# An encoder layer on one core: dividing attention outputs, not probabilities, by the softmax's sums

## The chip, the cores and the metric

The kernel runs on one core of a Trainium2 chip. The metric is device time in microseconds (us) of one launch, and lower is better. Three runs of the kernel before gave 1881.48, 1882.19 and 1882.21 us; the median is 1882.19 us.

## What is computed

One encoder layer with shared weights is applied to two groups of 512 tokens (g = 0 and 1). Its parts are an RMSNorm and a combined input projection; a bidirectional mLSTM; a multi-head attention with low-rank queries and keys; a gated merge of the two branches with an output projection; a SwiGLU feed-forward block; a gated embedding; a last RMSNorm. The change lies in the attention: 8 heads of 128 + 64 columns over 512 tokens, in float32.

```python
def mla_attention(q_nope, q_rope, k_nope, k_rope, v):
    scale = (A_NOPE + A_ROPE) ** -0.5
    ...
    def one(args):
        qn, qr = args
        s = jnp.einsum('bqhd,bkhd->bhqk', qn, k_nope) + jnp.einsum('bqhr,bkr->bhqk', qr, k_rope)
        p = jax.nn.softmax(s.astype(jnp.float32) * scale, axis=-1).astype(v.dtype)
        return jnp.einsum('bhqk,bkhd->bqhd', p, v)
```

The queries come from `rmsnorm(c_q, g_q) @ w_uq`, so a factor on the normed `c_q` is a factor on all queries, rotated ones too.

## The kernel before, in words

Activations stand as tiles of 128 features by 512 tokens. Every float32 operand of a matmul is split into a high part (a cast by ScalarE, `S.copy`) and a low part (a subtraction, `lo_of`, L154, mostly by VectorE), and a product is three matmuls: high by high, high by low, low by high.

The stages follow each other: input projections and mLSTM up to about 550 us, attention from about 580 to 862 us, then the products "mo" and "ao" (mLSTM and attention outputs by their weights, L1090), the output projection, feed-forward and the end. Tiles of one stage are stored to DRAM and loaded back by the next one where they don't fit.

Attention runs over 8 heads, and in each over the two groups: 16 pairs (hd, g). `attn_proj` (L773) makes a pair's queries, keys and values one head ahead: `qn` and `kn` by matmuls into PSUM banks "pj", their high and low parts (`qnl`, `knl`), the values from DRAM (`avt`, L787), their low part `vnl` on GpSimd (L788). On even heads the rotary part (`rope`, L741) adds eight VectorE instructions per group for two heads. `attn` (L791) then takes four blocks of 128 queries:

- 5 matmuls give the scores `sc` of 128 queries by 512 keys (L799 to L803) in one of three PSUM banks.
- VectorE finds each row's maximum (L805) and multiplies it by minus the scale (L806); ScalarE takes the exponential with that as bias, and its sums (L808); VectorE inverts the sum (L809); then the 128x512 block `p` is multiplied by it, on ScalarE (L811), or in block 1 on VectorE (L813).
- TensorE transposes `p` in four pieces into one of two banks `pt` (L816), and the result is split into `aph` (ScalarE, L818) and `apl` (VectorE, L154).

After the fourth block 12 matmuls (L823 to L825) multiply with the values into the bank `av`, ScalarE copies it to the tile `oz` (L827), and SyncE stores that to DRAM (L828), where "ao" finds it after the four "mo" products.

What else shares the engines in this stage: the merge gates (`merge_gate`, L695: 48 matmuls each, tiles `tg`) beside heads 0 to 3, and beside heads 4 to 6 the "hops", the operands of the product "mo": for k = 0 to 3 four tiles of the mLSTM's output are loaded (`ld<-hzd`, L1026, L832), subtracted from each other (L862 on VectorE, L865 on GpSimd) and split (`xh` L884, `xl` L154). Beside head 7 sixteen such tiles are loaded once more for the later operands (L1060), added on GpSimd (L868, L874, L875).

The pool EV has two slots "ch" and two slots "bk" of 128x512. In this stage "ch" holds `oz`, "bk" holds the gates' `tg` and two of the four hop tiles of each k (`stage`, L1021). A slot is given again when its last reader is done.

The order on each engine is not the program's: a scheduler sorts all instructions at build time, by its own model of their durations (`schedule_with_timeline_sim`, L1527), and each engine then works through its list in that order and waits where an operand is not there. SyncE's list (SP) is that of nearly all DMAs: a DMA whose source is not ready holds up all behind it.

Of the kernel before, what the change touches and what calls it, by code (L numbers as in the profile page):

```python
# [7 lines left out]
F32 = mybir.dt.float32  # L8
F32R = mybir.dt.float32r
I32 = mybir.dt.int32  # L10
AF = mybir.ActivationFunctionType
ALU = mybir.AluOpType
# [3 lines left out]
P = 128  # L16
T = 512
NB = T // P
G = 2
# [3 lines left out]
AH = 8  # L23
# [39 lines left out]
def encoder_kernel(ctx: ExitStack, tc: tile.TileContext, a):  # L63
    nc = tc.nc
# [20 lines left out]
    V, S, E, GP = (Engine(e) for e in (nc.vector, nc.scalar, nc.tensor, nc.gpsimd))  # L85
    cp = ctx.enter_context(tc.tile_pool(name="const", bufs=1))
    sm = ctx.enter_context(tc.tile_pool(name="sm", bufs=1))
    dr = ctx.enter_context(tc.tile_pool(name="dr", bufs=1, space=DRAM))
# [3 lines left out]
    def nm(s):  # L92
        ids[0] += 1
        return f"{s}_{ids[0]}"
# [14 lines left out]
    EV = Slots("EV", ch=2, bk=2)  # L109
# [19 lines left out]
    def bank(n="mm"):  # L129
        return pb[0](n)  # L130
# [7 lines left out]
    def col(name, i=0):  # L138
        o = COLS[name][0] + i
        return cols[:, o : o + 1]  # L140
# [8 lines left out]
    rcol = [cp.tile([P, 2 * NB], F32, name=f"rcol{g}") for g in range(G)]  # L149
# [3 lines left out]
    def lo_of(out, src, hi, e=V):  # L153
        e.tensor_tensor(out=out, in0=src, in1=hi.bitcast(F32), op=ALU.subtract)  # L154
# [63 lines left out]
    def sumsq(pc, sqs, b0=0, nb=NB):  # L218
        for i in range(nb):
            for k, q in enumerate(sqs):  # L220
                E.matmul(
                    pc[:, 2 * i : 2 * i + 2], q[:, (b0 + i) * P : (b0 + i + 1) * P], ones[:, 0:2],
                    start=k == 0, stop=k == len(sqs) - 1,
                )

    def spread(r, diag, b0=0, nb=NB):
        rh = sm.tile([P, 8], F32R, name=nm("rh"), tag="rh", bufs=2)[:, 0 : 2 * nb]
        V.tensor_copy(out=rh, in_=r)
        rl = sm.tile([P, 8], F32, name=nm("rl"), tag="rl", bufs=2)[:, 0 : 2 * nb]
        V.tensor_tensor(out=rl, in0=r, in1=rh.bitcast(F32), op=ALU.subtract)  # L230
        bc = bank("rbc")[:, b0 * P : (b0 + nb) * P]
        for i, v in enumerate((rh.bitcast(F32), rl)):
            dg = diag()[:, 0 : nb * P]
            V.tensor_tensor(
                out=dg.rearrange("p (a b) -> p a b", a=nb),
                in0=ident[:, None, :].to_broadcast([P, nb, P]),
                in1=v.rearrange("p (a b) -> p a b", b=2)[:, :, 0:1].to_broadcast([P, nb, P]),
                op=ALU.mult,
            )
            E.matmul(bc, onesr, dg, start=i == 0, stop=i == 1)  # L240
        return bc
# [81 lines left out]
    warm = bank("sT")  # L323
    for _ in range(WARM):
        E.matmul(warm, onesr, onesr[:, None, :].to_broadcast([P, NB, P]), start=True, stop=True)
# [144 lines left out]
    for i in range(NB):  # L470
        c = slice(i * P, (i + 1) * P)
        V.tensor_tensor_scan(
            out=M[:, c], data0=A[0][:, c], data1=A[0][:, c], initial=mprev[:, i : i + 1], op0=ALU.max, op1=ALU.max
# [4 lines left out]
    for d in range(1, NB):  # L478
        GP.tensor_copy(out=A[d][:, (NB - d) * P : T], in_=A[0][:, (NB - d) * P : T])
        for j in range(NB - d):  # L480
            e = (j + d) * P - 1
            V.tensor_scalar(
                out=A[d][:, j * P : (j + 1) * P],
                in0=A[d - 1][:, j * P : (j + 1) * P],
                scalar1=b[:, e : e + 1],
                scalar2=None,
                op0=ALU.add,
# [173 lines left out]
    def lat_norms():  # L661
        pairs = [(n, gn, g) for n, gn in (("ckv", "g_kv"), ("cq", "g_q")) for g in range(G)]
        pc = bank("ssc")
        for j, (n, gn, g) in enumerate(pairs):
            sq = [M1("tr", "sq") for _ in range(2)]
            for i in range(2):
                S.activation(out=sq[i], in_=early[f"{n}{i}", g], func=AF.Square)
            GP.tensor_tensor(out=sq[0], in0=sq[0], in1=sq[1], op=ALU.add)
            sumsq(pc[:, 8 * j : 8 * j + 8], sq[:1])
        ro = sm.tile([P, 32], F32, name="ro")  # L670
        for j, (n, gn, g) in enumerate(pairs):
            c = slice(8 * j, 8 * j + 8)
            V.tensor_tensor(out=ro[:, c], in0=pc[:, c], in1=rcol[g], op=ALU.mult)
            V.tensor_tensor(out=ro[:, c], in0=ro[:, c], in1=rcol[g], op=ALU.mult)
        r = rsqrt(ro, 32, 1.0 / 256)
        for j, (n, gn, g) in enumerate(pairs):
            c = slice(8 * j, 8 * j + 8)
            V.tensor_tensor(out=r[:, c], in0=r[:, c], in1=rcol[g], op=ALU.mult)
            bc = spread(r[:, c], lambda: M1("tr", "diag", F32R))
            for i in range(2):  # L680
                t = early[f"{n}{i}", g]
                V.scalar_tensor_tensor(out=t, in0=t, scalar=col(gn, i), in1=bc, op0=ALU.mult, op1=ALU.mult)
# [38 lines left out]
    for half in range(2):  # L721
        whi, wlo = weight(a["wv"][half])
        for g in range(G):
            for i in range(NB):
                bk = bank()
                for k in range(2):
                    n = slice(T * k, T * k + T)
# [5 lines left out]
                S.copy(t, bk)  # L733
                nc.sync.dma_start(vd[g][half][i], t)
    ozd = [[dr.tile([P, T], F32, name=f"ozd{g}_{c}") for c in range(AH)] for g in range(G)]
    cos = Q.pool.tile([P, T], F32, name="cos")
    nc.sync.dma_start(cos, a["cos"])
    sin = Q.pool.tile([P, T], F32, name="sin")
# [20 lines left out]
    for g in range(G):  # L759
        gs = Q("tr", "gs")  # L760
        nc.sync.dma_start(gs[0:64], gsd[g])
        r = rope(gs, 2)
# [4 lines left out]
        for o in (0, 64):  # L767
            V.tensor_tensor(out=kl[o : o + 64], in0=r[0:64], in1=kh[0:64].bitcast(F32), op=ALU.subtract)
        kst.append((kh, kl))
    scale = (128 + 64) ** -0.5  # L770
    qst = [[None] * 2 for _ in range(G)]

    def attn_proj(hd, g, wa):  # L773
# [17 lines left out]
    def attn(hd, g, ops):  # L791
        (qh, ql), (nh, nl), (vh, vl), q2 = ops
        kh, kl = kst[g]
        ph = Q("ph", "aph", F32R, (P, NB, T))
        pl = Q("pl", "apl", F32R, (P, NB, T))
        for i in range(NB):
            c = slice(i * P, (i + 1) * P)
            bk = bank("sc")
            E.matmul(bk, qh[:, c], nh, start=True, stop=False)  # L799
            E.matmul(bk, qh[:, c], nl, start=False, stop=False)  # L800
            E.matmul(bk, ql[:, c], nh, start=False, stop=False)
            E.matmul(bk, q2[:, c], kh, start=False, stop=False)
            E.matmul(bk, q2[:, c], kl, start=False, stop=True)  # L803
            mx = sm.tile([P, 4], F32, name=nm("mx"), tag="mx", bufs=4)
            V.tensor_reduce(out=mx[:, 0:1], in_=bk, axis=mybir.AxisListType.X, op=ALU.max)  # L805
            V.tensor_scalar(out=mx[:, 1:2], in0=mx[:, 0:1], scalar1=-scale, scalar2=None, op0=ALU.mult)  # L806
            p = Q("p", "p")
            S.activation(out=p, in_=bk, func=AF.Exp, bias=mx[:, 1:2], scale=scale, accum_out=mx[:, 2:3])  # L808
            V.reciprocal(out=mx[:, 3:4], in_=mx[:, 2:3])  # L809
            if i != 1:  # L810
                S.activation(out=p, in_=p, func=AF.Copy, scale=mx[:, 3:4])  # L811
            else:
                V.tensor_scalar(out=p, in0=p, scalar1=mx[:, 3:4], scalar2=None, op0=ALU.mult)  # L813
            tp = bank("pt")
            for j in range(NB):
                E.transpose(tp[:, j * P : (j + 1) * P], p[:, j * P : (j + 1) * P], ident)  # L816
            tp3 = tp.rearrange("p (a b) -> p a b", a=NB)
            S.copy(ph[:, :, c], tp3)  # L818
            lo_of(pl[:, :, c], tp3, ph[:, :, c])
        ob = bank("av")  # L820
        for j in range(NB):
            c = slice(j * P, (j + 1) * P)
            E.matmul(ob, vh[:, c], ph[:, j], start=j == 0, stop=False)  # L823
            E.matmul(ob, vl[:, c], ph[:, j], start=False, stop=False)
            E.matmul(ob, vh[:, c], pl[:, j], start=False, stop=j == NB - 1)  # L825
        o = EV("ch", "oz")
        S.copy(o, ob)  # L827
        nc.sync.dma_start(ozd[g][hd], o)  # L828

    def load(src, sl=EV, tag="bk", n="ld"):  # L830
# [287 lines left out]
    def sums(g, b0=0, nb=NB):  # L1118
        pc[g] = bank("ssc")
        sumsq(pc[g], ss[g].sq, b0, nb)  # L1120
# [187 lines left out]
    def halves(c):  # L1308
        st = (WP, WX)[c % 2]("wst", "wst", F32, (P, 1024))
        nc.sync.dma_start(st, a["w8"][W8[f"pg{c}"]])  # L1310
        return [wsplit(st[:, j * T : (j + 1) * T]) for j in range(2)]
# [57 lines left out]
    def spread3(g, b0=0, nb=NB):  # L1369
        rs2[g] = spread_f32(r2[g], b0, nb)  # L1370

    for c in range(LEAD):
        w = halves(c)
        for g in range(G):
            embed(c, g, proj2(w, x3[g]))
    for c in range(LEAD, KD):
        embed(c, 0, proj2(halves(c), x3[0]))
    w = halves(LEAD)
    pinned[0] = True
    last, cs = None, list(range(LEAD, KD - 2))  # L1380
    for s, c in enumerate(cs):
        nxt = halves(c + 1)
        bk = proj2(w, x3[1], mid=(lambda: sums(0)) if s == 0 else (lambda: spread3(0)) if s == 1 else None)
# [12 lines left out]
    bk = [proj2(ws[0], x3[1], toks[0])]  # L1396
# [34 lines left out]


LEAD = 2
WARM = 9
HOPS = {(4, 0): 3, (4, 1): 3, (5, 0): 3, (5, 1): 3, (6, 0): 2, (6, 1): 2}
LATN = (3, 0)
# [94 lines left out]
```

## Time and profile before

| what | value |
|---|---|
| three runs | 1881.48, 1882.19, 1882.21 us |
| profiled execution | span 1884.6 us from first to last instruction; the page gives no other time of it |
| TensorE matmuls (PE) | 1846.2 us busy, 98% |
| VectorE (DVE) | 1234.4 us, 66% |
| ScalarE (ACT) | 885.5 us, 47% |
| GpSimd (POOL) | 374.5 us, 20% |
| attention | first score matmul at 581.0 us, last matmul with values at 860.8 us |

A row of the windows view gives, for one stretch of time, the busy time and the number of instructions of each engine, then the granted TensorE clock (PEclk, 1.00 is full speed), the busy share of the DMA engines and GB/s. A row of the groups view has a line, an engine, an operation, out<-in, shapes and a count; then the busy time and the mean ns of one; then the idle time just before them and what ended it. A row of the timeline has start, duration, line and operation, and in brackets the idle time before it with what ended it. A matmul's duration in these rows includes pipeline overlap with the next one, so the spacing of starts is its real cost.

### The profile page before, as it was taken

The numbers are of one execution on the slowest core, as the hardware profiler recorded it, in microseconds if no ns is written. First come the engines' busy times: TensorE is split into PE (matmuls) and PEld (weight loads), VectorE is DVE, ScalarE is ACT, GpSimd is POOL, SyncE is SP. The second block draws the span as 40 slices with busy tenths as digits, with TensorE's granted clock in tenths as the row PEclk, the third lists the DMA queues.
The fourth block names the chain that finished last, engine by engine and source line by source line (L and its number), as shares of the span: only waits on it lengthen the run. The fifth ranks groups of instructions, "written<-read, shape, count | busy, mean of one in ns | idle before, by whom it ended". The sixth has DMA issues, their size and how long they took to land.

```text
span 1884.6 us, 24479 instructions
## 1 busy us (share of the span) xinstructions
PE 1846.2 (98%) x8849; PEld 1535.3 (81%) x8849; DVE 1234.4 (66%) x2200; ACT 885.5 (47%) x1726; POOL 374.5 (20%) x281
## 2 busy tenths in 40 slices
PE   9999999999999999899999999999999999999996
PEld 7888898988887888677878888888888887888786
DVE  6747575836554667976897587444444568878756
ACT  6255465543444666775434355333433343434333
POOL 0000000100000000352050003665566523111000
PEclk9999999999999999999999999999999999999998
DMA  4111111112254222445565241332223346543332
GB/s 166 52 45 35 57 34 57 35 67 71 81 170 140 65 73 87 129 153 192 166 207 173 90 162 68 111 118 95 95 90 121 103 158 228 157 130 100 106 134 95
DMA packets 98377, 208.11 MB, mean 110 GB/s; under 512 B 10832, under 2 KB 21456, under 8 KB 98256
## 3 DMA queue, kind: packets, MB, share of 16 engines
q1 hardware_dynamic: 85600, 161.72, 25.8%
q10 hardware_dynamic: 12096, 43.00, 7.1%
q0 software_dynamic: 560, 1.84, 0.2%
q8 instruction: 69, 1.13, 0.2%
q14 instruction: 52, 0.43, 0.1%
HBM read 151.89 MB, written 54.10 MB: 109 GB/s over the span
## 4 chain that ended last, share of the span: by engine, by line
PE 85%; DVE 9%; DMA 3%; ACT 1%; issue 1%; SPq 0%; POOL 0%; ACTq 0%; DVEq 0%
PE b L956 13%; PE b L958 12%; PE b L957 12%; PE mm L183 7%; PE mm L185 7%; PE mm L184 7%; PE mm L79 3%; PE nm L633 3%; DVE xl L154 2%; PE mm L548 2%; PE mm L550 2%; PE mm L549 2%; PE pt L816 1%; PE mm L1322 1%; PE mm L1323 1%
## 5 line engine op out<-in xcount | busy, mean ns | idle before, releaser
L957 PE MATMUL b<-xl,wp 128*128 128x512 f32 x1148 | 448.1, 392 | 1.7 <-DVE xl L154 1.7
L956 PE MATMUL b<-xh,wp 128*128 128x512 f32 x1148 | 442.1, 393 | 6.6 <-ACT u L997 2.3
L958 PE MATMUL b<-xh,wp 128*128 128x512 f32 x1148 | 444.2, 392 | 0.4 <-DVE wp L154 0.4
L900 ACT CAST wp<-wst 128x512 fp32r<-128x512 f32 (+1 forms) x270 | 164.2, 612 | 307.3 <-PE b L958 258.9
L154 DVE TENSOR_TENSOR wp<-wst,wp 128x512 fp32r<-128x512 f32 (+1 forms) x270 | 235.6, 875 | 67.0 <-ACT wp L900 66.6
L956 PEld LDWEIGHTS b<-xh,wp 128*128 128x128 f32 x1148 | 216.1, 188 | 59.1 <-ACT wp L900 5.5
L957 PEld LDWEIGHTS b<-xl,wp 128*128 128x128 f32 x1148 | 216.0, 188 | 49.0 <-DVE xl L154 2.6
L958 PEld LDWEIGHTS b<-xh,wp 128*128 128x128 f32 x1148 | 215.8, 188 | 48.3 <-DVE wp L154 1.3
L183 PE MATMUL mm<-hh,whi 128*128 128x512 f32 x560 | 220.4, 394 | 0.6 <-ACT raw L79 0.3
L184 PE MATMUL mm<-hl,whi 128*128 128x512 f32 x560 | 219.5, 392 | 0.0
L185 PE MATMUL mm<-hh,wlo 128*128 128x512 f32 x560 | 219.3, 392 | 0.0
L1002 DVE TENSOR_TENSOR u<-b,u 128x512 f32<-128x512 f32 x90 | 61.7, 689 | 132.5 <-PE b L958 82.6
L168 ACT CAST whi<-wst 128x1024 fp32r<-128x1024 f32 (+1 forms) x69 | 71.0, 1029 | 114.4 <-PE mm L184 69.6
L183 PEld LDWEIGHTS mm<-hh,whi 128*128 128x128 f32 x560 | 105.6, 189 | 23.3 <-ACT raw L79 0.8
L185 PEld LDWEIGHTS mm<-hh,wlo 128*128 128x128 f32 x560 | 105.5, 188 | 21.9
L184 PEld LDWEIGHTS mm<-hl,whi 128*128 128x128 f32 x560 | 105.6, 189 | 21.4
L927 POOL TENSOR_TENSOR s<-wst,wst 128x512 f32<-128x512 f32 (+1 forms) x30 | 47.4, 1579 | 321.9 <-DMA wst<-w 87.3
L154 DVE TENSOR_TENSOR wlo<-wst,whi 128x1024 fp32r<-128x1024 f32 (+1 forms) x69 | 83.1, 1204 | 30.9 <-ACT whi L168 30.5
L997 ACT COPY u<-b 128x512 f32<-128x512 f32 x90 | 50.8, 589 | 98.0 <-PE b L958 70.7
L1220 POOL TENSOR_TENSOR sg<-sg,u 128x512 f32<-128x512 f32 x30 | 54.6, 1819 | 203.3 <-DVE u L1002 203.3
L154 DVE TENSOR_TENSOR xl<-ld,xh 128x512 fp32r<-128x512 f32 x121 | 89.1, 764 | 7.0 <-ACT xh L884 6.2
L154 POOL TENSOR_TENSOR vnl<-avt,vnh 128x512 fp32r<-128x512 f32 x16 | 21.2, 1322 | 309.9 <-ACT vnh L158 251.4
(357 smaller groups left out, 3621.4 us busy)
## 6 DMA issues: line engine op xcount, KB each, us to landing
wst<-w SPq DMA_DIRECT2D x73, 512.0 KB
wst<-w ACTq DMA_DIRECT2D x60, 512.0 KB
ld<-actd SPq DMA_DIRECT2D x77, 256.0 KB
actd<-t SPq DMA_DIRECT2D x40, 256.0 KB
x<-x SPq DMA_DIRECT2D x32, 256.0 KB
ld<-hzd SPq DMA_DIRECT2D x32, 256.0 KB
wst<-wd ACTq DMA_DIRECT2D x16, 512.0 KB
actd<-sg SPq DMA_DIRECT2D x30, 256.0 KB
```

The costliest lines, as they stand in the source:

```text
L79: r = f(*args, **kw)
L154: e.tensor_tensor(out=out, in0=src, in1=hi.bitcast(F32), op=ALU.subtract)
L168: S.copy(hi[:, :n], st[:, :n])
L183: E.matmul(bk, whi[:, c], hi, start=k == 0, stop=False)
L184: E.matmul(bk, whi[:, c], lo, start=False, stop=False)
L185: last_mm[0] = E.matmul(bk, wlo[:, c], hi, start=False, stop=k == nk - 1)
L633: E.matmul(bk, l, r, start=n == 0, stop=n == len(terms) - 1)
L900: S.copy(hi, src)
L956: E.matmul(bk, whi[:, c], hi, start=bool(first) and k == 0, stop=False, **sk)
L957: E.matmul(bk, whi[:, c], lo, start=False, stop=False, **sk)
L958: E.matmul(bk, wlo[:, c], hi, start=False, stop=k == self.kh - 1, **sk)
L1002: V.tensor_tensor(out=t, in0=b, in1=t, op=ALU.add if name == "P2" else ALU.subtract)
```

## The change

The scale moves out of the softmax: it is multiplied into the 128x8 reciprocal norms of `c_q` in `lat_norms`. The maximum is negated by the reduction itself, the exponential has no scale, and its result is transposed undivided. The four sums of a pair are gathered in one 128x4 tile `den`; after the fourth block one reciprocal makes `rden`, which goes to DRAM as 4 rows of 128 (`rsd`, 512 pieces of 4 bytes) and comes back as one row of 512 given to all 128 partitions (`rb`, in a slot "bk"). After the values' product GpSimd multiplies `oz` by `rb` in place, and then it is stored.

```diff
@@ lat_norms
-            V.tensor_tensor(out=r[:, c], in0=r[:, c], in1=rcol[g], op=ALU.mult)
+            V.scalar_tensor_tensor(
+                out=r[:, c], in0=r[:, c], scalar=SCALE if n == "cq" else 1.0, in1=rcol[g], op0=ALU.mult, op1=ALU.mult
+            )
@@ attn
+        mx, den, rden = (sm.tile([P, NB], F32, name=nm(n), tag=n, bufs=2) for n in ("mx", "den", "rden"))
...
-            mx = sm.tile([P, 4], F32, name=nm("mx"), tag="mx", bufs=4)
-            V.tensor_reduce(out=mx[:, 0:1], in_=bk, axis=mybir.AxisListType.X, op=ALU.max)
-            V.tensor_scalar(out=mx[:, 1:2], in0=mx[:, 0:1], scalar1=-scale, scalar2=None, op0=ALU.mult)
+            V.tensor_reduce(out=mx[:, i : i + 1], in_=bk, axis=mybir.AxisListType.X, op=ALU.max, negate=True)
             p = Q("p", "p")
-            S.activation(out=p, in_=bk, func=AF.Exp, bias=mx[:, 1:2], scale=scale, accum_out=mx[:, 2:3])
-            V.reciprocal(out=mx[:, 3:4], in_=mx[:, 2:3])
-            if i != 1:
-                S.activation(out=p, in_=p, func=AF.Copy, scale=mx[:, 3:4])
-            else:
-                V.tensor_scalar(out=p, in0=p, scalar1=mx[:, 3:4], scalar2=None, op0=ALU.mult)
+            S.activation(out=p, in_=bk, func=AF.Exp, bias=mx[:, i : i + 1], accum_out=den[:, i : i + 1])
...
+        V.reciprocal(out=rden, in_=den)
+        nc.sync.dma_start(rsd[g][hd].rearrange("a p -> p a"), rden)
+        rb = EV("bk", "rb")
+        nc.sync.dma_start(rb, rsd[g][hd].rearrange("a p -> (a p)")[None, :].to_broadcast([P, T]))
         ob = bank("av")
...
         S.copy(o, ob)
+        GP.tensor_tensor(out=o, in0=o, in1=rb, op=ALU.mult)
         nc.sync.dma_start(ozd[g][hd], o)
```

`rsd` are new DRAM tiles (one per pair), and `SCALE` is (128 + 64) ** -0.5. New line numbers stand one to three higher than the old ones.

The scheduler sorts anew from the start of attention on. The first place is VectorE's list late in attention: the subtraction `ld<-ld,ld` (old L862, new L863) and the two splits `xl` of the hop tile k = 3 (`ld_8284` before, `ld_8188` now); `mx` are row maxima, `apl` low parts of transposed probabilities, `qs` rotated queries, `wp` weights. Before:

```order
L780 TENSOR_TENSOR qs_1360_7960<-rp_7952,qs_1360_7960 64x512
L805 TENSOR_REDUCE mx_8028<-sc_8022 128x1
L781 TENSOR_TENSOR qs_1361_7961<-rp_7952,qs_1361_7961 64x512
L862 TENSOR_TENSOR ld_8284<-ld_8284,ld_8286 128x512
L154 TENSOR_TENSOR wp_8510<-wst_8506,wp_8510 128x512
L154 TENSOR_TENSOR wp_8564<-wst_8506,wp_8564 128x512
L813 TENSOR_SCALAR p_7878<-p_7878,mx_7875 128x512
L154 TENSOR_TENSOR apl_7681<-pt_7755,aph_7680 128x4x128
L809 RECIPROCAL mx_7895<-mx_7895 128x1
L806 TENSOR_SCALAR mx_8028<-mx_8028 128x1
L809 RECIPROCAL mx_7915<-mx_7915 128x1
L154 TENSOR_TENSOR xl_8291<-ld_8284,xh_8289 128x512
```

And now the same hop tile:

```order
L807 TENSOR_REDUCE mx_8296<-sc_8333 128x1
L863 TENSOR_TENSOR ld_8188<-ld_8188,ld_8190 128x512
L154 TENSOR_TENSOR apl_8210<-pt_8252,aph_8209 128x4x128
L807 TENSOR_REDUCE mx_8296<-sc_8349 128x1
L154 TENSOR_TENSOR xl_8195<-ld_8188,xh_8193 128x512
L154 TENSOR_TENSOR apl_8210<-pt_8268,aph_8209 128x4x128
L816 RECIPROCAL rden_8298<-den_8297 128x4
L154 TENSOR_TENSOR xl_8200<-ld_8188,xh_8198 128x512
L154 TENSOR_TENSOR apl_8300<-pt_8310,aph_8299 128x4x128
L154 TENSOR_TENSOR apl_8300<-pt_8326,aph_8299 128x4x128
```

The last hop tile stood among the instructions of pairs (5, 0) to (6, 0), and now stands between the transposed blocks of the last two pairs, (7, 0) (`apl_8210`) and (7, 1) (`apl_8300`).

The second place is SyncE's list around that tile's load (`ld<-hzd_3`). `avt` are values, `ozd` stored attention outputs, `tmd` gates. Before:

```order
L828 DMA ozd_4_5718<-oz_7626 128x512
L832 DMA ld_8286<-hzd_7_804 128x512
L787 DMA avt_7988<-vd_5533 128x4x128
L787 DMA avt_8140<-vd_5531 128x4x128
L832 DMA ld_8284<-hzd_3_800 128x512
L1017 DMA ld_8581<-tmd_0_4809 128x512
```

And now:

```order
L833 DMA ld_8522<-hzd_7_796 128x512
L819 DMA rb_8141<-rsd_6_5736 128x512
L833 DMA ld_8525<-hzd_7_804 128x512
L833 DMA ld_8915<-ozd_0_5706 128x512
L833 DMA ld_8921<-ozd_1_5707 128x512
L833 DMA ld_8927<-ozd_2_5708 128x512
L833 DMA ld_8933<-ozd_3_5709 128x512
L829 DMA ozd_6_5712<-oz_8026 128x512
L833 DMA ld_8188<-hzd_3_800 128x512
L817 DMA rsd_7_5729<-rden_8208 128x4x1
L829 DMA ozd_6_5720<-oz_8156 128x512
L819 DMA rb_8277<-rsd_7_5729 128x512
```

The load moved from before the sixteen loads of head 7 to behind them, behind the reload `rb` of pair (6, 1) and behind the store of pair (6, 0), which itself waits for GpSimd's new multiplication. Behind the end of attention the lists agree with those before but for line and tile numbers and the places of some loads.

More of the change, by code (lines that the diff above doesn't have):

```diff
@@ L735, in encoder_kernel @@
     ozd = [[dr.tile([P, T], F32, name=f"ozd{g}_{c}") for c in range(AH)] for g in range(G)]
+    rsd = [[dr.tile([NB, P], F32, name=f"rsd{g}_{c}") for c in range(AH)] for g in range(G)]
     cos = Q.pool.tile([P, T], F32, name="cos")
@@ L769, in encoder_kernel @@
         kst.append((kh, kl))
-    scale = (128 + 64) ** -0.5
     qst = [[None] * 2 for _ in range(G)]
@@ L1433 @@
 LEAD = 2
+SCALE = (128 + 64) ** -0.5
 WARM = 9
```

## The prediction

> **What bounds the kernel now.** I read the windows view first, since TensorE is 98% busy over the whole span and only a stage where it isn't can give anything. The columns after the window's length are PE, PEld, DVE, ACT and POOL, then the granted clock.
>
> ```profile
> 600.00:650.00 50.00, 50.00 (x240) 41.51 (x238) 26.32 (x52) 26.31 (x51) 2.59 (x2) 1.00 0.24 79
> 700.00:750.00 50.00, 50.00 (x243) 41.41 (x242) 34.17 (x68) 29.88 (x59) 2.60 (x2) 1.00 0.25 79
> 575.00:759.00 184.00, 183.41 (x872) 150.71 (x871) 118.96 (x236) 107.27 (x208) 15.16 (x12) 1.00 0.27 86
> 759.00:811.00 52.00, 44.43 (x206) 34.73 (x205) 49.51 (x102) 38.12 (x79) 15.43 (x12) 0.98 0.36 111
> 811.00:865.00 54.00, 50.43 (x239) 39.39 (x239) 35.20 (x79) 41.05 (x88) 20.69 (x16) 0.95 0.40 142
> ```
>
> Up to 759 us TensorE loses 0.6 us: there the work removed lies under merge-gate matmuls and is worth nothing. In the third stretch, 759 to 811, PE is idle for 52.00 - 44.43 = 7.6 us, and VectorE is busy for 49.51 of 52: it is the bound there. In the last stretch PE loses 54.00 - 50.43 = 3.6 us with VectorE far from full. All that the change can win in attention is therefore about 11 us of idle PE, plus what a low clock costs.
>
> TensorE's waits between 575 and 870 us name who ended them (total, times, longest):
>
> ```profile
> PE sc L799 <- ACT p L808: 4.5, 5, 2.4
> PE av L825 <- DVE apl L154: 2.0, 1, 2.0
> PE pt L816 <- DVE apl L154: 1.9, 4, 0.7
> PE pj L183 <- DVE qnl L154: 1.9, 3, 0.9
> PE av L823 <- ACT aph L818: 0.7, 1, 0.7
> ```
>
> The first row is scores waiting for a PSUM bank that the exponential still reads, and the exponential waits for VectorE's maximum. The second is the stall at 806 us. The windows behind it show what an idle gap costs besides:
>
> ```profile
> 805.00:810.00 5.00, 3.03 (x12) 2.14 (x11) 5.00 (x10) 1.73 (x3) 3.88 (x3) 0.90 0.18 52
> 810.00:815.00 5.00, 4.85 (x20) 3.52 (x19) 3.14 (x8) 3.59 (x9) 0.38 (x1) 0.75 0.13 50
> ```
>
> The clock drops to 0.75, and the timeline shows six matmuls in a row (the first and the last of them) at a spacing of (811.17 - 809.05) / 5 = 0.42 us, against 0.23 us in the two rows at 799 us:
>
> ```profile
> 799.62 0.40 PE L802 MATMUL sc<-kh,qs 128*128 128x512 f32 x1
> 799.85 0.39 PE L803 MATMUL sc<-kl,qs 128*128 128x512 f32 x1
> 809.05 0.62 PE L823 MATMUL av<-aph,vnh 128*128 128x512 f32 x1
> 811.17 0.63 PE L825 MATMUL av<-apl,vnh 128*128 128x512 f32 x1
> ```
>
> That is 6 x 0.19 = 1.2 us. The stretch loses 7.6 + 1.2 = 8.8 us in all.
>
> **The change part by part.** VectorE in the saturated stretch, by group (count, busy us and mean ns, idle before):
>
> ```profile
> L805 DVE TENSOR_REDUCE mx<-sc 128x1 f32<-128x512 f32 x15 | 10.1, 678 | 0.1
> L154 DVE TENSOR_TENSOR xl<-ld,xh 128x512 fp32r<-128x512 f32 x13 | 9.5, 729 | 0.1
> L862 DVE TENSOR_TENSOR ld<-ld,ld 128x512 f32<-128x512 f32 x4 | 2.8, 704 | 3.1 <-DMA ld<-hzd 3.1
> L813 DVE TENSOR_SCALAR p<-p,mx 128x512 f32<-128x512 f32 x3 | 2.4, 814 | 0.0
> L809 DVE RECIPROCAL mx<-mx 128x1 f32<-128x1 f32 x14 | 2.1, 153 | 0.1
> L806 DVE TENSOR_SCALAR mx<-mx 128x1 f32<-128x1 f32 x16 | 2.1, 139 | 0.0
> ```
>
> *Removed from VectorE.* L813 goes (2.4 us) and L806 (2.1 us). Of 14 reciprocals about 4 remain, each now 128x4, which no row shows; by the nearest row, 128x1, 10 x 0.153 = 1.5 us go. That is 6.0 us of busy time. But small instructions overlap their neighbours:
>
> ```profile
> 774.84 0.14 DVE L806 TENSOR_SCALAR mx<-mx 128x1 f32<-128x1 f32 x1
> 774.90 0.15 DVE L809 RECIPROCAL mx<-mx 128x1 f32<-128x1 f32 x1
> 774.97 0.13 DVE L806 TENSOR_SCALAR mx<-mx 128x1 f32<-128x1 f32 x1
> ```
>
> Start to start they take 0.065 us, so the lower bound is 2.4 + 26 x 0.065 = 4.1 us, and I take that one, as VectorE hardly idles here and starts are what counts. The negated reduction writes the same 128x1 from the same 128x512, so I cost it as L805: 0.68 us, no change.
>
> *Moved on VectorE.* The stretch also holds most of the hops: 13 `xl` and 4 subtractions, 9.5 + 2.8 = 12.3 us. The new order puts those of k = 3 among the last two pairs and those of k = 2 by pair (6, 0), where VectorE had room (35.20 of 54.00 us). I count a third moved out, 4 us. VectorE's load falls to 49.5 - 4.1 - 4 = 41.4 us, under TensorE's 44.4 - 1.2 = 43.2 us at full clock. Two engines so close still wait for each other at times; I let a quarter of the loss remain: **-8.8 x 0.75 = -6.6 us**. The bounds are -8.8 (all of it) and -4.1 (only what VectorE gives up directly).
>
> *Removed from ScalarE.* Over the whole of attention:
>
> ```profile
> L811 ACT ACTIVATE p<-p,mx 128x512 f32<-128x512 f32 x48 | 34.5, 737 | 16.1 <-DVE mx L809 12.9 <-DVE mx L806 3.2
> ```
>
> 34.5 us, nearly all beside PE's work. It counts where TensorE waits for the exponential behind it. After 811 us that happens twice:
>
> ```profile
> 836.57 0.50 PE L799 MATMUL sc<-knh,qnh 128*128 128x512 f32 x1 [0.56 <-ACT p L808]
> 847.17 0.50 PE L799 MATMUL sc<-knh,qnh 128*128 128x512 f32 x1 [0.27 <-ACT p L808]
> 854.18 0.66 PE L816 MATMUL pt<-ident,p 128*128 128x128 f32 x4 [0.74 <-DVE apl L154]
> ```
>
> Those two go: **-0.8 us**. The third kind stays: transposes in a row wait for `aph` and `apl` to empty the two `pt` banks, and the new order keeps three in a row before the last 12 matmuls.
>
> *GpSimd's multiplication.* 16 instructions, SBUF by SBUF. Nearest row: the low part of the values, same shape.
>
> ```profile
> L154 POOL TENSOR_TENSOR vnl<-avt,vnh 128x512 fp32r<-128x512 f32 x16 | 21.2, 1322 | 309.9 <-ACT vnh L158 251.4 <-PE pt L816 44.0 <-DVE mx L809 14.4
> ```
>
> 16 x 1.32 = 21 us on an engine that is idle for hundreds. `vnl` of a later pair queues behind it, but a full pair's time ahead of need. The cost is what it does to VectorE, which these rows show:
>
> ```profile
> 768.40 0.48 DVE L813 TENSOR_SCALAR p<-p,mx 128x512 f32<-128x512 f32 x1
> 805.86 1.49 DVE L813 TENSOR_SCALAR p<-p,mx 128x512 f32<-128x512 f32 x1
> 805.42 1.65 POOL L930 TENSOR_TENSOR wst<-wst,wst 128x512 f32<-128x512 f32 x1 [8.42 <-DVE wp L154]
> ```
>
> Beside a GpSimd instruction one VectorE instruction took 1.0 us longer. In this stretch that is rare: L813's three cost 3 x (0.814 - 0.48) = 1.0 us over their normal, `xl` 13 x (0.729 - 0.68) = 0.6, so 1.6 us over POOL's 12 instructions, 0.13 us each. Four multiplications fall here and one or two near them; with some room for instructions that I haven't counted, 0.2 us each: **+1.0 us**. The bounds are 0 and 5 x 1.32 = 6.6 us. The Trainium skill, "SBUF — State Buffer", section "Who interferes with whom", has a rule against this change: a VectorE instruction with two SBUF inputs and a GpSimd instruction that reads SBUF share a port under an exclusive lock, and the later one blocks for the whole instruction. The 1.49 us above agrees with such a lock; by that rule taken at its worst the term would be an estimated 6.6 us, and the sum lies near zero.
>
> *The two transfers.* The prices of the write in 4-byte pieces and of the broadcast are shown by no row. Nearest ones are single steps of the chain of waits for a 256 KB load, and the wait of a hop on its load:
>
> ```profile
> 765.06 2.71 DMA ld<-hzd
> 831.04 5.26 DMA ld<-hzd
> 759.60 0.75 DVE L862 TENSOR_TENSOR ld<-ld,ld 128x512 f32<-128x512 f32 x1 [2.39 <-DMA ld<-hzd]
> 824.86 9.10 SPq L832 DMA_DIRECT2D ld<-hzd x16
> ```
>
> So 2.7 to 5.3 us for each, 5.4 to 10.5 us for the round trip, and I take 8. The multiplication needs it only after the pair's last 12 matmuls, some 6 us after the last exponential in pair (7, 1) and 10 to 20 us in the others, and no matmul waits for `oz`. Early on the slots "bk" pass from `rb` to gates `tg` with several us to spare. What queues behind the waits on SyncE is the point: `rb` can't be issued until `rsd` has landed, so SyncE stands for 2.7 to 5.3 us per pair, with weights, values and hop tiles behind. Weights and values are issued tens of us ahead. Hop tiles aren't: already now VectorE stood 2.39 us for one. The hop of k = 3 is issued behind sixteen loads (9.10 us of issue), a reload and a store that waits for GpSimd. I put its landing some 15 us before the end of attention, and VectorE reaches its subtraction some 12 us before the end: an estimated slack of 3 us. For all hops I take **+1.3 us**, with bounds of 0 and 8 (2 us at each of k = 0 to 3).
>
> *The rest.* Four 128x8 instructions in `lat_norms` take a constant more: no change. After attention nothing is changed but for loads shifted by a few us, with PE full there.
>
> The sum: -6.6 - 0.8 + 1.0 + 1.3 = **-5.1 us**. It is made against the span of 1884.6 us, which the shown runs undercut by 2.4 us (median 1882.19); stalls of attention are the same in both, so 1882.2 - 5.1 = **1877.1 us**. A measurement of this kernel tells a change from none at about 0.2%, 3.8 us.
>
> **The rivals.**
>
> A, *the gain is given back*. Only the 4.1 us come back, and hop loads take 3 us: -4.1 - 0.8 + 1.0 + 3 = -0.9, 1881.3 us. For it: the hops' DMAs already stall VectorE. Against: VectorE loses far more work than it waited. Chance 0.21.
>
> B, *SyncE's queue becomes the bound, and it is slower*. The place is the hop loads behind `rsd` and `rb`. If the 4-byte write takes x us longer than the 5.3 of the slowest row, each hop comes x later; 2 us of slack at k = 0 to 2 and about none at k = 3, as VectorE's subtraction stands between the last transposed blocks: 3 (x - 2) + x. It decides from x = 3.1, where 4x - 6 = 6.4 eats the other terms (-6.6 - 0.8 + 1.0). At x = 4.7, a write of 10 us, it is +12.8 - 6.4 = +6.4, 1888.6 us. Against: it needs a write of over 8 us. The Trainium skill, "DMA: Bandwidth & Descriptors", section "Specifications", speaks for it: transfers in pieces below 512 B are slowed by read-modify-write; no row of this trace has such a write. Chance 0.16.
>
> C, *the port lock at its worst*: 6.6 instead of 1.0, -5.1 + 5.6 = +0.5, 1882.7 us. Of 12 GpSimd instructions in the stretch few blocked anything. Chance 0.06.
>
> **How the numbers follow.** The forecast has 0.57, and is faster. A and C are within 0.2%: 0.27. B is slower: 0.16. The best case regains 8.8 + 0.8 at no cost: 1872.6. The range takes in A, C and the nearer part of B: 1872 to 1886 us.
>
> **What would show it.** Right: 759 to 811 us without VectorE at 95%, the waits on `p` L808 down, no clock below 0.9 before the last transposes, PE idle in attention down from 11 to about 6 us. Rival B would show waits of VectorE on `ld<-hzd` and SyncE waiting on `rsd`; C long `xl` and `wlo` beside GpSimd's multiplication. I am wrong if attention ends later, or if PE's idle time appears in the part before 759 us.

## The result, and the profile after

The changed kernel takes 1912.76 us (median of 4 runs, 1911.74 to 1913.9), against 1881.84 us before (4 runs, 1877.26 to 1882.21): 30.9 us more. The ratio is 1.017, with a 95% interval of 1.0155 to 1.0184. The prediction was 1877.1 us, in a range that ended at 1886. The profiled execution spans 1912.0 us, 27.4 more than the one of before.

The same stretches of the windows view (PE, PEld, DVE, ACT, POOL busy; granted clock; DMA share; GB/s), and one more behind them, show where the time went:

```profile
575.00:759.00 184.00, 182.58 (x862) 149.10 (x862) 105.41 (x161) 87.00 (x176) 23.38 (x18) 1.00 0.33 89
759.00:811.00 52.00, 37.19 (x161) 29.53 (x160) 34.52 (x55) 23.58 (x52) 11.87 (x9) 0.87 0.32 76
811.00:865.00 54.00, 43.01 (x184) 33.58 (x182) 32.38 (x52) 29.96 (x66) 18.32 (x14) 0.87 0.53 131
865.00:925.00 60.00, 50.77 (x225) 40.40 (x224) 33.79 (x49) 26.05 (x52) 23.34 (x17) 0.91 0.69 207
```

VectorE did come down, from 49.51 to 34.52 us in the stretch from 759 to 811 us, and is no longer the bound; yet TensorE is idle there for 14.8 us instead of 7.6. Attention now ends after 890 us. From 575 to 925 us, a window of each kernel, before and then after, gives the sum:

```profile
575.00:925.00 350.00, 338.27 (x1576) 274.09 (x1575) 247.65 (x481) 212.39 (x420) 61.83 (x44) 0.99 0.36 119
```

```profile
575.00:925.00 350.00, 313.55 (x1426) 252.61 (x1426) 206.10 (x314) 166.60 (x344) 76.91 (x58) 0.95 0.42 114
```

PE's idle time there grew from 11.7 to 36.4 us: 24.7 of the 27.4 us. TensorE, VectorE and ScalarE do less in this window; GpSimd does 15.1 us more, but is busy for only 76.9 of the 350. So the cause isn't work. From the first score matmul to the first matmul of "mo" it is 280.0 us before (581.0 to 861.0) and 314.6 now (580.0 to 894.6): all of the loss, and more, lies in attention. SyncE's own waits have a new first row (us in total, times, longest), and the hops' waits on their loads grew beside it, as does TensorE's wait for blocks behind them:

```profile
SPq L819 <- DMA rsd<-rden: 120.3, 16, 11.0
```

```profile
POOL oz L828 <- DMA rb<-rsd: 43.1, 6, 10.2
ACT xh L885 <- DMA ld<-hzd: 24.0, 7, 6.7
POOL s L928 <- DMA wst<-w: 15.8, 1, 15.8
PE pt L812 <- DVE apl L154: 13.3, 6, 6.5
PE sc L802 <- ACT p L809: 8.9, 2, 8.2
```

SyncE stands at the 16 broadcast loads for 7.5 us each until the reciprocals have landed. A quiet place of its timeline gives the price of one write from its issue:

```profile
652.83 0.37 SPq L817 DMA_DIRECT2D rsd<-rden  x1
661.27 0.33 SPq L819 DMA_DIRECT2D rb<-rsd  x1
```

That is 8.4 us, near the least of the 16; the most is 11.45 (761.44 to 772.89). The DMA view of these 8.5 us, in 40 slices, shows that the packets themselves take little of it:

```profile
DMA  0000470000000000000000000000000000000000
GB/s 0 0 0 0 4 6 0 0 0 0 0 0 0 0 0 0 0 0 0 0 0 0 0 0 0 0 0 0 0 0 0 0 0 0 0 0 0 0 0 0
DMA packets 528, 0.00 MB, mean 0 GB/s; under 512 B 528, under 2 KB 528, under 8 KB 528
```

All 528 packets go out within about 0.4 us, and then nothing moves for 7 us until the write counts as landed. All this looks like rival B, SyncE's queue. One place does not fit it. The longest stall of TensorE, 8.15 us at 775.73, goes back over ScalarE and GpSimd to a weight load (two pieces of the timeline; in brackets, the idle time before and its releaser):

```profile
760.76 0.33 ACTq L914 DMA_DIRECT2D wst<-w  x1
772.60 1.26 POOL L928 TENSOR_TENSOR s<-wst,wst 128x512 f32<-128x512 f32 x1 [15.80 <-DMA wst<-w]
773.89 0.62 ACT L901 CAST wp<-s 128x512 fp32r<-128x512 f32 x1 [9.85 <-POOL s L928]
775.73 0.79 PE L802 MATMUL sc<-knh,qnh 128*128 128x512 f32 x1 [8.15 <-ACT p L809]
```

That load was issued on ScalarE's queue, 0.7 us before a write of reciprocals (761.44) and so before SyncE stood for it. It took 11.8 us to its first use; before, the same one took 4.8 us:

```profile
752.30 0.33 ACTq L913 DMA_DIRECT2D wst<-w  x1
757.14 1.29 POOL L927 TENSOR_TENSOR s<-wst,wst 128x512 f32<-128x512 f32 x1 [1.57 <-DMA wst<-w]
```

And in the DMA view of the changed kernel from 755.5 to 775.5 us, slices of 0.5 us, nothing at all moves between 766.0 and 774.0, while the write (761.44 to 772.89) is on its way:

```profile
DMA  9997980000177596989430000000000000000446
GB/s 424 401 354 254 373 307 25 0 0 0 61 209 266 160 217 119 324 340 224 144 71 0 0 0 0 0 0 0 0 0 0 0 0 0 0 0 0 156 106 213
```

SyncE issued nothing between its write and 772.89, so the empty stretch alone does not show that anything was held up. The weight load does show it. From 760.7 to 766.2 us ScalarE's queue has this row:

```profile
q10 hardware_dynamic: 144, 0.52, 35.3%
```

These are all packets of the load (512 KB), and none follows up to 774 us. Yet GpSimd could use it only at 772.60, 0.3 us before the write was counted as landed. So what came late here is not the load's bytes but its landing.

### The profile page after: what moved, and what is told of

Same layout as the page of the kernel before. It is cut to its first block, busy times and chain, and to the rows that moved or that the text cites. A ratio compares the mean times of both kernels' runs of the same rounds, so it can differ in the third digit from the quotient of the medians.

```text
span 1912.0 us, 24422 instructions
## 1 busy us (share of the span) xinstructions
PE 1847.7 (97%) x8849; PEld 1540.7 (81%) x8849; DVE 1214.4 (64%) x2072; ACT 856.2 (45%) x1678; POOL 396.2 (21%) x297
## 4 chain that ended last, share of the span: by engine, by line
PE 46%; DVE 6%; DMA 3%; issue 1%; ACT 1%; SPq 0%; POOL 0%; ACTq 0%; DVEq 0%
PE b L957 12%; PE b L959 12%; PE b L958 12%; PE mm L79 2%; DVE xl L154 1%; PE mm L185 1%; PE mm L183 1%; PE mm L184 1%; DMA rsd<-rden 1%; PE mm L1322 1%; PE mm L1323 1%; PE mm L1324 1%; DMA ld<-hzd 1%; DVE wp L154 1%; DMA wst<-wd 0%
## 5 line engine op out<-in xcount | busy, mean ns | idle before, releaser
L154 DVE TENSOR_TENSOR wp<-wst,wp 128x512 fp32r<-128x512 f32 (+1 forms) x270 | 228.3, 848 | 68.8 <-ACT wp L901 68.4
```

## The experiments

Four theories stood at the start. **W**: SyncE's wait for the write holds up what is issued behind it (rival B). **P**: the write's small pieces hold up other transfers, on any queue. **O**: the new places of hops and projections among the last pairs cost the time by themselves. **G**: GpSimd's multiplication does, by slowing VectorE. A fifth, **S**, came later: the broadcast tile takes one of the two slots that the hop loads need. The order of TensorE, VectorE and ScalarE was the changed kernel's in the runs e4, e8 and e9, and e1, e5, e6, e7, e10 and e11 have one order among them (e7 but for two rows), which differs from it in 49, 31 and 25 places on the three engines.

**e1, without the wait.**

```diff
-        nc.sync.dma_start(rb, rsd[g][hd] ... to_broadcast([P, T]))
+        old = rsd[last[0][0]][last[0][1]].rearrange("a p -> (a p)")[None, :] if last[0] else a["cos"][0:1, :]
+        last[0] = (g, hd)
+        nc.sync.dma_start(rb, old.to_broadcast([P, T]))
```

> The broadcast load of a pair reads the sums of the pair before it in the program (the first pair reads a row of the cosines), so it need not wait for its own write; the write, the load, the slots and the multiplication stay. It divides by another pair's sums. Theory W (the wait): SyncE stands 120.3 us at the 16 broadcast loads for the write to land, and the hop loads, values and stores behind them come late; without it the time falls to 1877 to 1885 us and the wait at the broadcast load is under 10 us. Theory O (the order): the changed places of hops and projections among the last pairs cost the time; these rows are nearly the same here, so 1905 to 1914. Theory P (the pieces): the 512 pieces of 4 bytes of each write hold up other transfers; 1905 to 1914, as they are still written. Theory G (the multiplication on GpSimd slows VectorE): 1905 to 1914.

Measured: 1906.51 us, ratio 1.0129 (1.0112 to 1.0145). SyncE stood 36.3 us at the broadcast load, not 120.3, and a fifth of the loss came back. Not the end of W, since some standing was left, but a first blow.

**e2, both transfers on GpSimd's queue.**

```diff
-        nc.sync.dma_start(rsd[g][hd] ..., rden)
+        GP.dma_start(rsd[g][hd] ..., rden)
-        nc.sync.dma_start(rb, ...)
+        GP.dma_start(rb, ...)
```

> The write of the reciprocals and the broadcast load are issued by GpSimd instead of SyncE; everything is still computed. Theory W: SyncE no longer stands for the write, 1877 to 1885 us; GpSimd stands instead, with the low parts of the values and the hop sums behind it, which costs 0 to 4 us of that. Theories O, P and G: the pieces, the multiplication and nearly all of the order are still there, 1905 to 1914.

Measured: 1925.56 us, ratio 1.0231 (1.0214 to 1.0248): worse than any theory said. SyncE's waits say where the standing went:

```profile
SPq L829 <- POOL oz L828: 128.5, 14, 25.5
```

GpSimd now stands for the write, its multiplication comes late, and SyncE waits for that at the store of the output, with the same hop loads behind. The wait was moved, not removed, so this run does not tell W from P.

**e3, the division left out** (no write, no broadcast load, no multiplication).

> The division is left out: no write, no broadcast load, no multiplication. Theory W: the floor of what the removed work can bring, 1870 to 1880 us. Theory P: the same. Theory G: the same. Theory O: the hops stand among the last pairs as in the changed kernel, 1900 to 1914.

Measured: 1873.62 us against 1881.8, ratio 0.9951 (0.9934 to 0.9969). It is 8 us faster than the kernel before. It says nothing on O, since its hops do not stand where the changed kernel has them: the last subtraction follows the 43rd of 64 transposed blocks, as before (804.04 us), and not the 58th as in the changed kernel (878.91 us):

```profile
801.47 0.68 DVE L859 TENSOR_TENSOR ld<-ld,ld 128x512 f32<-128x512 f32 x1
```

**e4, the write in 128 pieces of 16 bytes.**

```diff
-        nc.sync.dma_start(rsd[g][hd].rearrange("a p -> p a"), rden)
+        nc.sync.dma_start(rsd[g][hd].rearrange("a p -> (a p)").rearrange("(p a) -> p a", a=NB), rden)
```

> The write goes to DRAM in 128 pieces of 16 bytes instead of 512 of 4 bytes; the sums are then divided out in another order than they belong to. On TensorE, VectorE, ScalarE and GpSimd the order is the changed kernel's, row for row. Theory W: the write lands in an estimated 2.5 to 5 us after issue instead of 8 to 11, SyncE's standing falls from 120 us to 35 to 75 us, and the time to 1883 to 1900. Theory P: a quarter of the pieces, a quarter of the loss, 1885 to 1892. Theories O and G: 1910 to 1914.

Measured: 1876.68 us against 1881.8, ratio 0.9973 (0.9963 to 0.9983). The write, the wait, the load and the multiplication are all there, in the changed kernel's order, and the loss is gone. SyncE's wait for the write is 22.0 us in all; the place that took 8.4 us takes 2.2:

```profile
650.86 0.32 SPq L817 DMA_DIRECT2D rsd<-rden  x1
653.10 0.32 SPq L819 DMA_DIRECT2D rb<-rsd  x1
```

This rules out O and G, and leaves W and P: with a write that lands soon SyncE hardly stands, and others are not held up.

**e5, e6, e7: no write, a write that nothing reads, and that write on another queue.** In all three the broadcast load reads a row of the cosines, so the division by the sums is left out and nothing waits for the write.

```diff
-        nc.sync.dma_start(rb, rsd[g][hd] ... to_broadcast([P, T]))
+        nc.sync.dma_start(rb, a["cos"][0:1, :].to_broadcast([P, T]))
-        nc.sync.dma_start(rsd[g][hd] ..., rden)     # e5: left out; e6: kept
+        GP.dma_start(rsd[g][hd] ..., rden)          # e7
```

> The reciprocals are not written; the broadcast load reads a row of the cosines, which has long been in DRAM, and the multiplication is by that row. The division by the sums is left out. If the write is the cause (theory W or P), 1875 to 1882 us, at the level of the run with long pieces (1876.7) or a little lower. Theory S (the broadcast tile holds one of the two slots that the hop loads need): 1895 to 1908, since the slots are as before.

> As the run without the write, but the write in 4-byte pieces is issued by SyncE as in the changed kernel, and nothing reads it. TensorE, VectorE and ScalarE have the same order in both. Theory W (only SyncE's standing costs): 1875 to 1884 us, as nothing stands for the write now. Theory P (what is issued behind the write crawls until it has landed: in the run with another pair's sums 0.64 MB took some 10 us behind one): 1893 to 1908.

> As the run without the write, but the write in 4-byte pieces is issued by GpSimd, on a queue of its own, and nothing reads it. If the crawl is in SyncE's queue alone: 1875 to 1884 us. If it is in what the queues share (the DMA engines or the memory): 1890 to 1908. Theory W: 1875 to 1884.

Measured: e5 1875.99 us, ratio 0.9975 (0.996 to 0.9991); e6 1906.16, 1.0138 (1.0121 to 1.0156); e7 1906.47, 1.0136 (1.0121 to 1.0151). So S falls with e5. The write costs 30 us by being there, though nothing reads it, and the same from either queue. W is left with the step from e6 to the changed kernel, 6.6 us by the medians and 6.0 by the ratios; the two intervals just touch (1.0156 and 1.0155), and the orders differ a little, so this is an upper bound more than a price. e1, in e6's order row for row and with 36.3 us of SyncE's standing left, takes the same time as e6. The waits of ScalarE for hop loads, in e5 and in e6:

```profile
ACT xh L884 <- DMA ld<-hzd: 5.8, 3, 4.0
```

```profile
ACT xh L885 <- DMA ld<-hzd: 23.2, 5, 9.5
```

**e10, the same 512 pieces of 4 bytes, each 64 bytes from the next.**

```diff
-    rsd = [[dr.tile([NB, P], F32, ...
+    rsd = [[dr.tile([NB, P, 16], F32, ...
-        nc.sync.dma_start(rsd[g][hd].rearrange("a p -> p a"), rden)
+        nc.sync.dma_start(rsd[g][hd][:, :, 0:1].rearrange("a p o -> p a o"), rden.rearrange("p (a o) -> p a o", o=1))
```

> As the run with the unused write (1906.2 us), order for order, but each of the 512 pieces of 4 bytes goes to an address of its own 64 bytes from the next, so that no two pieces lie close together. If the number of pieces or their size is what costs, 1900 to 1908 us as there. If it is that 16 neighbouring pieces hit the same 64 bytes, 1875 to 1884, at the level without a write (1876.0).

Measured: 1876.91 us against 1880.97, ratio 0.998 (0.9971 to 0.9989). As many pieces, as small, on the same queue, in e6's order row for row: the 30 us are gone. SyncE's rows at the same place of the program, in e6 and in e10, show what a write does to the two loads behind it:

```profile
774.93 0.37 SPq L817 DMA_DIRECT2D rsd<-rden  x1
776.21 0.32 SPq L833 DMA_DIRECT2D ld<-hzd  x1
777.59 0.33 SPq L819 DMA_DIRECT2D rb<-cos  x1
787.43 0.32 SPq L829 DMA_DIRECT2D ozd<-oz  x1
```

```profile
768.91 0.37 SPq L817 DMA_DIRECT2D rsd<-rden  x1
770.20 0.32 SPq L833 DMA_DIRECT2D ld<-hzd  x1
771.58 0.33 SPq L819 DMA_DIRECT2D rb<-cos  x1
775.93 0.32 SPq L829 DMA_DIRECT2D ozd<-oz  x1
```

From the broadcast load to the store of the product (which waits for the load and the multiplication) it is 9.8 us in e6 and 4.4 in e10. The DMA view of the 10 us from the write's issue agrees: 0.97 MB at 97 GB/s in e6, 1.64 MB at 164 GB/s in e10. Part of that is that e6 issues less here, 3 transfers against 6. But the two loads, issued by 777.9, crawl: in e6's row of 40 slices of 0.25 us, no slice from 779.9 to 784.6 is above 90 GB/s.

```profile
GB/s 221 328 360 279 442 150 70 50 49 221 83 115 8 16 0 49 0 8 0 147 90 74 90 82 90 74 33 90 57 49 49 49 74 57 49 57 25 25 57 115
DMA packets 930, 0.97 MB, mean 97 GB/s; under 512 B 577, under 2 KB 577, under 8 KB 930
```

```profile
DMA packets 1371, 1.64 MB, mean 164 GB/s; under 512 B 616, under 2 KB 724, under 8 KB 1371
```

**e11, a quarter of the pieces** (one of a partition's four reciprocals, 128 pieces of 4 bytes side by side; nothing reads them).

```diff
-        nc.sync.dma_start(rsd[g][hd].rearrange("a p -> p a"), rden)
+        nc.sync.dma_start(rsd[g][hd][0:1].rearrange("a p -> p a"), rden[:, 0:1])
```

> As the run with the unused write, but only one of the four sums of a partition is written: 128 pieces of 4 bytes instead of 512, side by side as before. If each small piece has its price, a quarter of the 30 us: 1880 to 1888. If a write has a price however many pieces it has, 1898 to 1908. As many pieces of 16 bytes cost next to nothing (1876.7): if it is the size of a piece and not their number, 1895 to 1908 as well.

Measured: 1899.35 us (1895.66 to 1904.02), ratio 1.0101 (1.0084 to 1.0118). A quarter of the pieces has about three quarters of the cost, so it is no price per piece. What e11 shares with e6 is 16 pieces of 4 bytes in each 64 bytes; e4 has 4 in 64, e10 one.

**e12, the fold alone** (the diff's first part and `negate=True`; the probabilities are divided as before).

> Only the scale goes into the queries and the maximum is negated in the reduction; the probabilities are divided by their sums as before. VectorE loses 64 instructions of 128x1 at 0.065 us from start to start, 1 us of them in the saturated stretch: 1879 to 1881.5 us against before's 1881.5, a gain of 0 to 2.5. If the gain of leaving the division out (1873.6) came from the fold, 1874 to 1877.

Measured: 1881.69 us, ratio 1.0004 (0.9995 to 1.0013): nothing. So the 8 us of e3 do not come from the fold. Where they lie is looked at further down.

**e8 and e9, two whole kernels with long pieces.** The 16-byte pieces bring the sums to DRAM in another order. Both have e4's write. e8 makes that order right by taking every fourth query into a block; e9 by reading the broadcast tile with a stride in GpSimd's multiplication.

```diff
+            c = slice(i, T, NB)                                      # e8, for slice(i * P, (i + 1) * P)
+        GP.tensor_tensor(                                            # e9, for in0=o, in1=rb
+            out=o.rearrange("p (a q) -> p a q", a=NB),
+            in0=o.rearrange("p (a q) -> p a q", a=NB),
+            in1=rb.rearrange("p (q a) -> p a q", a=NB),
+            op=ALU.mult,
+        )
```

> Everything is computed. A block of queries is every fourth query instead of 128 neighbours, so that the sums of a partition's four queries stand side by side and the write has 128 pieces of 16 bytes. Orders are the changed kernel's but for SyncE's. Theories W and P: as with long pieces, 1875 to 1879 us. If TensorE's weights with a stride of 16 bytes, or ScalarE's and VectorE's strided writes of the transposed blocks, are slower than unstrided ones by a tenth, 2 to 8 us more.

> Everything is computed. The write has 128 pieces of 16 bytes, as in the run with long pieces, and GpSimd's multiplication puts the order right by reading the broadcast tile with a stride of four elements. TensorE, VectorE and ScalarE keep the changed kernel's order and shapes. If the short pieces are the whole cause, 1875 to 1879 us, faster than before by 3 to 6 us. If the strided operand doubles GpSimd's 1.32 us (as the strided writes of the transposed blocks nearly doubled, 0.59 to 1.10 us on ScalarE), some 0 to 2 us more.

Measured: e8 1894.46 us, ratio 1.0071 (1.0058 to 1.0083). Its strides cost far more than a tenth; ScalarE's copy of the transposed blocks and a weight load, in e4 and in e8:

```profile
L814 ACT CAST aph<-pt 128x512 fp32r<-128x512 f32 x64 | 37.6, 592 | 29.4 <-PE av L824 16.3 <-PE pt L812 12.9
...
L803 PEld LDWEIGHTS sc<-knl,qnh 128*128 128x128 f32 x64 | 12.1, 189 | 1.5
```

```profile
L814 ACT CAST aph<-pt 128x512 fp32r<-128x512 f32 x60 | 65.3, 1098 | 25.1 <-PE av L824 16.0 <-PE pt L812 8.9
...
L803 PEld LDWEIGHTS sc<-knl,qnh 128*128 128x128 f32 x64 | 20.4, 320 | 0.3
```

e9: 1877.47 us (11 runs) against 1880.97 (27 runs), 3.5 us less by the medians; the ratio, 0.9992 (0.9982 to 1.0001), does not tell it from before. It undoes the loss and is 35 us faster than the changed kernel, but whether it beats the kernel before is not settled. Its multiplication takes longer, 1582 ns against 1322 in e4:

```profile
L828 POOL TENSOR_TENSOR oz<-oz,rb 128x512 f32<-128x512 f32 x16 | 25.3, 1582 | 44.5 <-ACT oz L827 44.5
```

## Why the prediction was wrong, point by point

*What bounds the kernel, and what the removed work is worth*: the size came out, by luck; the mechanism did not. The two terms were -6.6 and -0.8, together -7.4 us, all of it in attention. e3 gave 8.2 by the medians (5.8 to 12.4 by its interval), but its profile has most of that elsewhere. A row of the tiles view names the first and the last start of a group: `sc` are the scores, `b` the products behind attention. Before, e3 and e4:

```profile
L799 PE MATMUL sc<-knh,qnh x64: 389/395/500, 581.0 to 847.2; 128*128 128x512 f32 x64
L956 PE MATMUL b<-xh,wp x1148: 387/389/628, 861.0 to 1776.3; 128*128 128x512 f32 x192
```

```profile
L802 PE MATMUL sc<-knh,qnh x64: 389/397/504, 579.9 to 844.5; 128*128 128x512 f32 x64
L953 PE MATMUL b<-xh,wp x1148: 387/389/505, 857.0 to 1764.2; 128*128 128x512 f32 x192
```

```profile
L802 PE MATMUL sc<-knh,qnh x64: 389/394/499, 578.7 to 841.5; 128*128 128x512 f32 x64
L957 PE MATMUL b<-xh,wp x1148: 387/389/504, 859.8 to 1766.5; 128*128 128x512 f32 x192
```

Attention, from the first `sc` to the first `b`, takes 280.0 us before, 277.1 in e3 and 281.1 in e4 (279.0 to 281.5 in e5, e9 and e10). From the first `b` to the start of the last it is 915.3 us before, 912.7 in e12, 907.2 in e3 and 906.7 in e4. So e3, whose hops stayed, shows 2.9 us of the 7.4 in attention, and the kernels with the moved hops show about none: TensorE's idle time from 759 to 865 us, 11.1 us before, is 14.6 in e4 and 12.0 in e10. In e4 there is less of it up to 811 us, 5.3 instead of 7.6, and more behind, 9.3 instead of 3.6: with the hops, the waits moved to the end. The gain lies where the prediction saw no change ("After attention nothing is changed but for loads shifted by a few us, with PE full there"). About 3 us of it is a drop of the clock that only the profiles of before (0.66 from 1590 to 1595 us) and of the changed kernel have there. The rest is that the same matmuls follow each other more closely: the first 300 behind attention start 228.5 ns apart before and 228.6 in e12, but 226.7 in e3, e10 and the changed kernel. Why is open. There is one profile of each kernel, so these parts are less sure than the medians.

*GpSimd's multiplication*: about right. It and the broadcast load together are the step from e3 to e5: 2.4 us by the medians, 4.5 by the ratios (0.9975 against 0.9951). The term for the multiplication was +1.0. The port lock at its worst (rival C), 6.6 us for the multiplication alone, has no place in this. But such a lock shows in the traces, as here in e5:

```profile
846.69 1.26 POOL L827 TENSOR_TENSOR oz<-oz,rb 128x512 f32<-128x512 f32 x1
846.71 1.80 DVE L154 TENSOR_TENSOR xl<-ld,xh 128x512 fp32r<-128x512 f32 x1
```

An `xl`, with two inputs in SBUF, takes 0.68 us alone. Three of them overlap a multiplication in e5 (0.94, 1.80 and 1.43 us) and lose 2.1 us in all; the low parts `apl`, with one input in PSUM, take 0.68 to 0.69 us beside it as elsewhere. So rival C had the mechanism, and it met three instructions in attention.

*The two transfers*: this is the step that failed. "So 2.7 to 5.3 us for each", and from it "+1.3 us, with bounds of 0 and 8". The transfers' whole price is the step from e5 to the changed kernel, 36.8 us. It failed twice. The duration was taken from loads of 256 KB, as if a small transfer could only be quicker: the write took 8.4 to 11.5 us. And the sum asked only who stands behind SyncE's wait; it took for granted that a transfer of 2 KB does nothing to other transfers. Of the 36.8 us SyncE's wait is worth at most about 6.6 (e6 to the changed kernel), and 30.2 is the mere presence of the write (e5 to e6).

*Rival B* had the sign, and its condition, a write of over 8 us, was met. But its mechanism is the lesser part: by its own sum a write of 10 us gives 1888.6 us, and taking SyncE's wait away (e6) left the kernel at 1906. The rule of the Trainium skill cited for it, on pieces below 512 B in "DMA: Bandwidth & Descriptors", section "Specifications", pointed at the right transfer; but by e10 pieces of 4 bytes cost nothing when they lie 64 bytes apart, and by e4 pieces of 16 bytes nothing when they lie side by side. Nor is it so that no row before has a write in such pieces: `lfd<-lf` writes 32 KB in 128 pieces of 256 bytes, and the load that reads it is issued 2.8 us after it. That row would have given the price that the prediction took, and no warning.

```profile
57.50 0.34 SPq L443 DMA_DIRECT2D lfd<-lf  x1
60.28 0.62 SPq L450 DMA_DIRECT2D rfn<-lfd  x2
```

*The scale fold and the rest*: no change, as e12 shows.

With the write mended and nothing else (e4) the ratio is 0.9973, 5.1 us below the time before. That this is the -5.1 of the sum is luck: e4's attention is no shorter than that of the kernel before, and its gain lies behind attention.

What stays open: why neighbouring 4-byte pieces do this. The runs show that it is not their number (e10, e11), the queue (e7), or a wait on them (e6). Whether the 16-byte pieces are cheap for their size or because only four of them share 64 bytes was not told apart, nor how far apart small pieces must lie: e10 also spreads each write over 32 KB instead of 2.

## What to carry to other kernels

A transposing write of 2 KB to DRAM in 4-byte neighbours can cost far more than its bytes suggest: 16 of them cost 30 us here, and the cost falls on other transfers, those of other queues too. Look at the pieces of a transfer, not at its bytes, and write what lies together in a partition as one piece; put the order right where it is cheap, in one strided operand off the critical path. When a new transfer seems to hurt through a wait, keep the transfer and take only the wait away: here that told 6.6 us from 30. And when a gain has the size that was forecast, look whether it lies where it was forecast: here it did not.

## What the runs showed of the hardware

- 512 pieces of 4 bytes, 16 to each 64 bytes of DRAM, went out within about 0.4 us where nothing else moved, and counted as landed 8.4 to 11.5 us after issue. A weight load on another queue whose packets were over by 766.2 us could be used only at 772.6. 64 bytes apart, the same pieces cost nothing that could be measured.
- A VectorE instruction with two inputs in SBUF took 1.80 us beside a GpSimd multiplication, 0.68 alone.
- A stride of 16 bytes on 4-byte elements: ScalarE's 128x512 copy 592 to 1098 ns, TensorE's 128x128 weight load 189 to 320 ns, GpSimd's multiplication with one strided input 1322 to 1582 ns.
- The granted clock was low behind a long gap: 0.64 from 774 to 784 us, around the end of the stall of 8.15 us.

```profile
774.00:784.00 10.00, 8.27 (x29) 6.71 (x30) 8.53 (x13) 7.68 (x17) 2.89 (x3) 0.64 0.41 139
```
